# Hybrid decoder trunk on one core: the small transfers of gate offsets, router and gate columns held in program order

## The chip, the core and the metric

The kernel runs on one core of a Trainium2 chip. Its time is the device time of one execution in microseconds (us); lower is better. TensorE (PE) multiplies, VectorE (DVE) and ScalarE (ACT) do elementwise work, GpSimd (POOL) a few small things, and SyncE (SP) only issues transfers. ACT issues transfers too, between its other instructions. Transfers of SP run on the queue that the profile calls q1, those of ACT on q10.

## The reference, cut to what matters

Two layers on 256 tokens of width 1024. Each has a token mixer and a channel mixer (dense in layer 0, eight experts with a router in layer 1). The change touches the mixer's two small gate projections and constants beside them:

```python
p = h @ w_in
qk, v, o, ig, fg, cb, cc, cx, ga, gb = jnp.split(p, _split_points(), axis=-1)
qk = jax.nn.silu(causal_depthwise_conv(qk, conv_qk))
i_pre = (ig + b_gates[:H]).transpose(0, 2, 1)      # 4 heads: gate columns and gate offsets
f_pre = (fg + b_gates[H:]).transpose(0, 2, 1)
hm = mlstm_chunkwise(heads(q), heads(k) * (Dh ** -0.5), heads(v), i_pre, f_pre)
...
logits = (t @ w_router).astype(jnp.float32)        # layer 1 only
```

## The kernel before, in words

All products are made in three passes from a high and a low float32r part of each operand. Weights arrive as 1 MB units through SP into a ring of four buffers, `raw` (numbers 79 to 82 in the program's order). Each unit gives two halves. ACT casts a half to `hi` (line 121), DVE makes `lo` from the rest (line 123), both in rings of seven (hi_83 to hi_89, lo_90 to lo_96). PE then uses them.

The start, layer 0: the conditioning products (`ada_acc`, lines 275 and 277, sums on DVE in `accs`; `ada_col`, line 290 on PE and 292 on DVE, result `adac`) need four `w_ada` units and the table `badaT`, which PE turns (line 231) out of `prow`, a small transfer of ACT. `adac` scales the tokens: PE turns them (line 407), ACT and DVE apply the scale (399, 401), and the parts `h_hi`, `h_lo` (lines 80 and 81) go into the first large products (476 to 478, 464 to 466).

`mixer` then works through `w_in` in groups of 512 columns. After the first q/k group, `params()` has brought small tables: `prm` (convolution weights and norms, turned by PE at line 231 and copied at 232), the gate offsets `bg` (four transfers of 4 numbers each) and the router weights `wr` (128 partitions with eight runs of 8 numbers). `gates()` then borrows the next `hi` and `lo` tile (hi_89, lo_96) for the gate columns: a transfer brings `graw`, ACT casts it (502), DVE makes the low part (503), and PE makes 24 products (506 to 508). A chain of small steps on ACT and DVE follows, ending in `grow`, which PE turns at line 529 after the next group. In layer 1 the same `gates()` follows the last product for v.

A scheduler sets each engine's order from priorities and an estimate of readiness. It may move an instruction far ahead of where the code stands, unless it is wrapped in `tc.keep_in_program_order`, which keeps it behind the instructions of its engine that the code issued earlier. Completion of transfers is signalled on eight semaphores (DMAHW0 to DMAHW7 in the program's order), taken in turn by the transfers of both queues. A transfer waits until the earlier one on its semaphore has landed.

Of the kernel before, what the change touches and what calls it, by code (L numbers as in the profile page):

```python
# [46 lines left out]
def trunk(ctx: ExitStack, tc: tile.TileContext, x, c, w_ada, b_ada, w_in, w_gates, b_gates, conv_qk,  # L47
          hn_gain, conv_short, w_out, ln_g, ln_b, dense_w13, dense_w2, w_router, moe_w13,
          moe_w2, out):
    nc = tc.nc  # L50
# [12 lines left out]
    def bank(shape=(128, 512), name="bank"):  # L63
        return psum.tile(list(shape), F32, tag="bank", name=name)
# [21 lines left out]
    def turn(name):  # L86
        t = turns[name]
        t[0] += 1
        return t[1][t[0] % len(t[1])]
# [114 lines left out]
    def kview(w):  # L204
        return w.rearrange("(c p) n -> p c n", p=128)
# [20 lines left out]
    def rows_to_cols(t, n, srcs):  # L226
        r = small.tile([128, 512], F32, tag="hf", bufs=2, name="prow")[0:n, 0:128]
        for d, src in srcs:
            nc.scalar.dma_start(r[d], src)
        pt = bank()  # L230
        T.transpose(pt[:, 0:n], r, ident[0:n, 0:n])
        A.copy(t, pt[:, 0:n])
# [4 lines left out]
    bg = const.tile([64, 2], F32, name="bg")  # L237

    def params():
        V.memset(bg, 0.0)  # L240
        for l in range(2):
            rows_to_cols(prm[l], 128, [
                (slice(0, 64), conv_qk[l].rearrange("t (c p) -> (t c) p", p=128)),
                (slice(64, 88), conv_short[l].rearrange("t (c p) -> (t c) p", p=128)),
                (slice(88, 96), hn_gain[l].rearrange("(c p) -> c p", p=128)),
                (slice(96, 128), (ln_g, ln_b)[l].rearrange("l i (c p) -> (l i c) p", p=128))])
            if l == 1:
                nc.scalar.dma_start(wr, kview(w_router[0]))
            nc.scalar.dma_start(bg[0:4, l:l + 1], b_gates[l, 4:8].rearrange("(h o) -> h o", o=1))
            nc.scalar.dma_start(bg[32:36, l:l + 1], b_gates[l, 0:4].rearrange("(h o) -> h o", o=1))  # L250

    def lng_col(l, i):
        b = 96 + l * 16 + i * 8
# [3 lines left out]
    wr = const.tile([128, KC, NE], F32, name="wr")  # L257
# [233 lines left out]
    def gates(mix, l, hi, lo):  # L491

        gst_hi = turn("hi").rearrange("p (k m) -> p k m", m=128)
        gst_lo = turn("lo").rearrange("p (k m) -> p k m", m=128)
        G.memset(gst_hi.bitcast(F32), 0.0)
        G.memset(gst_lo.bitcast(F32), 0.0)
        grow = mix.tile([36, S], F32, name="grow")
        G.memset(grow, 0.0)
        gr = mix.tile([128, KC, 8], F32, name="graw")
        nc.scalar.dma_start(gr, w_gates[l])  # L500
        for src, dst in ((slice(4, 8), slice(0, 4)), (slice(0, 4), slice(32, 36))):
            A.copy(gst_hi[:, :, dst], gr[:, :, src])
            V.tensor_tensor(gst_lo[:, :, dst], gr[:, :, src], gst_hi[:, :, dst].bitcast(F32), op=OP.subtract)
        pg = bank()
        for k in range(KC):
            T.matmul(pg[:, 0:S], gst_hi[:, k], hi[:, k], start=k == 0, stop=False)
            T.matmul(pg[:, 0:S], gst_hi[:, k], lo[:, k], start=False, stop=False)
            T.matmul(pg[:, 0:S], gst_lo[:, k], hi[:, k], start=False, stop=k == KC - 1)

        f, e, bb, r = (mix.tile([4, S], F32, name=n) for n in ("gf", "ge", "gb", "gr"))  # L510
        M = f
        V.tensor_scalar(f, pg[0:4, 0:S], bg[0:4, l:l + 1], None, op0=OP.add)
        A.activation(r, pg[32:36, 0:S], AF.Identity, bias=bg[32:36, l:l + 1])
        V.scalar_tensor_tensor(e, f, -1.0, f, op0=OP.mult, op1=OP.min)
        A.activation(e, e, AF.Exp)
        A.activation(e, e, AF.Ln, bias=1.0)
        V.scalar_tensor_tensor(f, f, 0.0, e, op0=OP.min, op1=OP.subtract)
        V.tensor_tensor_scan(bb, ones[0:4, 0:1].to_broadcast([4, S]), f, 0.0, op0=OP.mult, op1=OP.add)
        V.tensor_tensor(r, r, bb, op=OP.subtract)
        V.tensor_tensor_scan(M, r, r, 0.0, op0=OP.max, op1=OP.max)  # L520
        V.tensor_tensor(e, bb, M, op=OP.add)
        V.tensor_copy(grow[0:4], r)
        A.activation(grow[32:36], e, AF.Exp, scale=-1.0)
        gcol = mix.tile([128, 2, 36], F32, name="gcol")

        def then():
            pc = bank((128, 2, 36))
            for tb in range(2):
                T.transpose(pc[:, tb], grow[:, tb * 128:tb * 128 + 128], ident[0:36, 0:36])
            V.tensor_copy(gcol, pc)  # L530
        return M, gcol, then
# [68 lines left out]
    def mixer(ctx, l, z, norms, Gc, Bc, xA, g1):  # L600
# [19 lines left out]
        if norms is None:  # L620
# [15 lines left out]
            for cg in range(2):  # L636
                for tb in range(2):
                    v_out(pvs[cg][tb], cg, tb)
            xA = xA(z)
            params()  # L640
        else:
            pvs = [[], []]
# [17 lines left out]
            background()  # L660
        lead[0] = AHEAD
        M, gcol, gates_then = gates(mix, l, hi, lo)
        q, k = t8("q"), t8("k")
        for gi in range(4):
# [917 lines left out]
```

## Time and profile before

| | |
|---|---|
| median of 3 runs | 1766.92 us (1766.28 to 1768.98) |
| the profiled execution, its own time | 1764.21 us |
| span in its trace | 1762.5 us |
| PE busy | 1669.0 us, 95% of the span |
| DVE, ACT, POOL busy | 1047.1, 719.6, 70.6 us |
| mean granted PE clock | 0.983 of full |

The span runs from the first to the last recorded instruction; the 1.7 us between it and the execution's own time lie around it. All rows below are of this one execution, in microseconds from the span's start.

### The profile page before, as it was taken

To read this page: it belongs to the slowest core of one execution; us is meant where nothing else is said; L and a number is where in the kernel's file an instruction comes from. 1 tells how busy PE (TensorE), PEld (TensorE's weight loads), DVE (VectorE), ACT (ScalarE), POOL (GpSimd) and SP (SyncE) were. 2 spreads that over 40 slices of the span, in tenths; PEclk is the share of its full clock that TensorE was granted. 3 is DMA by queue.
4 is the path that set the end of the run, shared out by engine and by line. 5 is a ranking of instruction groups with operands and counts; after the bars stand their busy time and mean duration, and the time that the engine had idled before them with its cause. 6 is when DMAs were issued, how large, how long until landed. Compare 5 with 4: busy or idle time off the path is not lost. (4 is left out here: it accounts for less than half of the span.)

```text
span 1762.5 us, 28144 instructions
## 1 busy us (share of the span) xinstructions
PE 1669.0 (95%) x11401; PEld 1282.6 (73%) x11401; DVE 1047.1 (59%) x1531; ACT 719.6 (41%) x975; POOL 70.6 (4%) x82
## 2 busy tenths in 40 slices
PE   5999998999998999997999999999999999999996
PEld 4899996999996999995776665555555555566662
DVE  7699858776567999758844644322323233555554
ACT  2774444544444764544633433222222222334440
POOL 0001002000003001003000000000000000000000
PEclk9999998999998999998999999999999999999998
DMA  8667753766663776662789999999899999999994
GB/s 342 222 250 267 263 181 123 283 249 253 229 236 123 286 268 256 242 229 107 263 330 416 411 397 376 373 403 380 352 419 364 393 393 411 392 366 421 421 420 175
DMA packets 78131, 541.16 MB, mean 307 GB/s; under 512 B 10057, under 2 KB 10409, under 8 KB 13225
## 3 DMA queue, kind: packets, MB, share of 16 engines
q1 hardware_dynamic: 74880, 534.81, 77.6%
q10 hardware_dynamic: 3112, 4.48, 0.7%
q8 instruction: 91, 1.49, 0.3%
q14 instruction: 48, 0.39, 0.1%
HBM read 538.20 MB, written 1.05 MB: 306 GB/s over the span
## 5 line engine op out<-in xcount | busy, mean ns | idle before, releaser
L123 DVE TENSOR_TENSOR lo<-raw,hi 128x1024 fp32r<-128x1024 f32 x376 | 449.7, 1220 | 162.7 <-ACT hi L121 162.2
L121 ACT CAST hi<-raw 128x1024 fp32r<-128x1024 f32 x382 | 389.8, 1048 | 273.3 <-PE grp L465 177.5
L464 PE MATMUL grp<-h_hi,hi 128*128 128x256 f32 x1408 | 401.8, 286 | 0.5 <-ACT hi L121 0.5
L466 PE MATMUL grp<-h_hi,lo 128*128 128x256 f32 x1408 | 397.7, 283 | 0.0
L465 PE MATMUL grp<-h_lo,hi 128*128 128x256 f32 x1408 | 397.5, 282 | 0.0
L464 PEld LDWEIGHTS grp<-h_hi,hi 128*128 128x128 f32 x1408 | 268.6, 191 | 2.9 <-issue 1.4
L465 PEld LDWEIGHTS grp<-h_lo,hi 128*128 128x128 f32 x1408 | 268.6, 191 | 2.0 <-issue 1.7
L466 PEld LDWEIGHTS grp<-h_hi,lo 128*128 128x128 f32 x1408 | 268.5, 191 | 0.0
L1132 DVE TENSOR_TENSOR ss<-bank,ss 128x256 f32<-128x256 f32 (+1 forms) x42 | 16.9, 402 | 236.7 <-PE bank L1085 236.7
L478 PE MATMUL bank<-lo,x_parts 128*128 128x512 f32 x336 | 137.2, 408 | 2.7 <-DVE lo L123 2.6
L476 PE MATMUL bank<-hi,x_parts 128*128 128x512 f32 x336 | 135.4, 403 | 2.8 <-ACT hi L121 2.8
L1130 ACT ACTIVATE ss<-bank 128x256 f32<-128x256 f32 (+1 forms) x42 | 15.4, 366 | 288.7 <-PE bank L1085 288.7
L477 PE MATMUL bank<-hi,x_parts 128*128 128x512 f32 x336 | 132.4, 394 | 0.0
L1085 PE MATMUL bank<-raw,x_pairs 128*64 128x256 f32 x1056 | 122.4, 385 | 0.0
L1085 PEld LDWEIGHTS bank<-raw,x_pairs 128*64 128x64 f32 x1056 | 74.3, 138 | 42.0 <-issue 3.4
L123 DVE TENSOR_TENSOR lo<-raw_moe,hi 128x1024 fp32r<-128x1024 f32 x76 | 89.5, 1220 | 25.0 <-ACT hi L121 24.9
L476 PEld LDWEIGHTS bank<-hi,x_parts 128*128 128x128 f32 x336 | 63.2, 188 | 31.7 <-ACT hi L121 19.5
L1085 PE MATMUL bank<-raw,mg 128*64 128x512 f32 (+1 forms) x432 | 85.6, 537 | 0.5 <-ACT mg L1145 0.5
L277 DVE SCALAR_TENSOR_TENSOR acc<-raw,cond,acc 128x512 f32<-128x512 f32 x120 | 83.7, 744 | 0.1
L121 ACT CAST hi<-raw_moe 128x1024 fp32r<-128x1024 f32 x76 | 76.3, 1050 | 14.7 <-PE bank L477 12.9
L478 PEld LDWEIGHTS bank<-lo,x_parts 128*128 128x128 f32 x336 | 63.0, 187 | 23.5 <-DVE lo L123 6.6
L1145 ACT COPY mg<-bank 128x256 f32<-128x256 f32 (+1 forms) x42 | 14.9, 355 | 158.3 <-PE bank L1142 158.3
(314 smaller groups left out, 2345.2 us busy)
## 6 DMA issues: line engine op xcount, KB each, us to landing
raw<-in_moe_w_dram SPq DMA_DIRECT2D x192, 1024.0 KB, 7.9
raw_moe<-in_moe_w_dram SPq DMA_DIRECT2D x96, 1024.0 KB, 7.2
raw<-in_w_in_dram SPq DMA_DIRECT2D x72, 1024.0 KB, 5.4
raw<-in_w_ada_dram SPq DMA_DIRECT2D x48, 1024.0 KB, 4.8
raw_big<-in_moe_w_dram SPq DMA_DIRECT2D x48, 1024.0 KB, 7.8
raw<-in_dense_w_dram SPq DMA_DIRECT2D x42, 1024.0 KB, 6.2
raw<-in_w_out_dram SPq DMA_DIRECT2D x8, 1024.0 KB, 5.8
g<-in_b_ada_dram SPq DMA_DIRECT2D x8, 256.0 KB
```

The source lines that it names most:

```text
L121: A.copy(hi, raw)
L123: V.tensor_tensor(lo, raw, hi.bitcast(F32), op=OP.subtract)
L277: V.scalar_tensor_tensor(a, raw[:, jj], cond[:, j:j + 1], a, op0=OP.mult, op1=OP.add)
L464: T.matmul(o, whi[:, kk, fs], hi[:, k], start=first, stop=False, skip_group_check=True)
L465: T.matmul(o, whi[:, kk, fs], lo[:, k], start=False, stop=False, skip_group_check=True)
L466: T.matmul(o, wlo[:, kk, fs], hi[:, k], start=False, stop=k == KC - 1, skip_group_check=True)
L476: T.matmul(o, ahi, whi, start=start, stop=False)
L477: T.matmul(o, alo, whi, start=False, stop=False)
L478: T.matmul(o, ahi, wlo, start=False, stop=stop)
L1085: T.matmul(o[c * p:c * p + p, 0:n], act, w[:, c * n:c * n + n], start=start, stop=stop)
L1130: A.activation(dst, src, AF.Silu)
L1132: V.tensor_tensor(dst, src, dst, op=OP.mult)
```

## The change

Six transfers are wrapped: the router weights, the four gate offsets (the two lines become a loop over the same two slices) and, in each layer, the gate columns. What is moved, and how many bytes, stays the same.

```diff
             if l == 1:
-                nc.scalar.dma_start(wr, kview(w_router[0]))
-            nc.scalar.dma_start(bg[0:4, l:l + 1], b_gates[l, 4:8].rearrange("(h o) -> h o", o=1))
-            nc.scalar.dma_start(bg[32:36, l:l + 1], b_gates[l, 0:4].rearrange("(h o) -> h o", o=1))
+                tc.keep_in_program_order(nc.scalar.dma_start(wr, kview(w_router[0])))
+            for ps, hs in ((slice(0, 4), slice(4, 8)), (slice(32, 36), slice(0, 4))):
+                tc.keep_in_program_order(
+                    nc.scalar.dma_start(bg[ps, l:l + 1], b_gates[l, hs].rearrange("(h o) -> h o", o=1)))
...
         gr = mix.tile([128, KC, 8], F32, name="graw")
-        nc.scalar.dma_start(gr, w_gates[l])
+        tc.keep_in_program_order(nc.scalar.dma_start(gr, w_gates[l]))
```

Lines below 249 have numbers one higher in the changed kernel. Three places of the order show what moves.

On SP at the start, with the semaphores that each transfer waits for, before:

```order
L114 DMA raw_80<-in_w_ada_dram 128x2048
L114 DMA raw_81<-in_w_ada_dram 128x2048
L114 DMA raw_82<-in_w_ada_dram 128x2048
L114 DMA raw_79<-in_w_ada_dram 128x2048 [waits DMAHW4_49]
L114 DMA raw_80<-in_w_in_dram 128x2048 [waits DMAHW5_49,DMAHW1_49,DVE_49]
```

and in the changed kernel:

```order
L114 DMA raw_80<-in_w_ada_dram 128x2048
L114 DMA raw_81<-in_w_ada_dram 128x2048
L114 DMA raw_82<-in_w_ada_dram 128x2048
L114 DMA raw_79<-in_w_ada_dram 128x2048
L114 DMA raw_80<-in_w_in_dram 128x2048 [waits DMAHW1_49,DVE_49]
```

The order is the same; the fourth load no longer waits for a semaphore that a transfer of ACT's held.

On ACT in layer 0, from the copies of the two `prm` tables on. Before, where the six transfers stand far ahead, five of them at the start of the program and the sixth behind `badaT`:

```order
L232 COPY prm_120<-bank 128x128
L232 COPY prm_121<-bank 128x128
L541 ACTIVATE q<-cpad_132,prm_120 128x256 x2
L536 COPY cpad_133<-grp 128x2x256
L541 ACTIVATE q<-cpad_133,prm_120 128x256 x2
L121 CAST hi_89<-raw_81 128x1024
L513 ACTIVATE gr<-bank,bg 4x256
```

and in the changed kernel:

```order
L232 COPY prm_120<-bank 128x128
L251 DMA bg<-in_b_gates_dram 4x1 x2
L232 COPY prm_121<-bank 128x128
L248 DMA wr<-in_w_router_dram 128x8x8
L251 DMA bg<-in_b_gates_dram 4x1 x2
L501 DMA graw<-in_w_gates_dram 128x64
L542 ACTIVATE q<-cpad_132,prm_120 128x256 x2
L537 COPY cpad_133<-grp 128x2x256
L542 ACTIVATE q<-cpad_133,prm_120 128x256
L503 CAST hi_89<-graw 128x8x4 x2
```

All six transfers and the cast of the gate columns now stand behind the copy of `prm_120`. PE's order here is unchanged: the two turns of `prm` (line 231), then the 24 gate products that read hi_89, then the next group.

On ACT in layer 1, around the copies of v. Before, where `graw` was asked for some 340 us earlier:

```order
L617 COPY v_ext<-bank 128x2x256
L502 CAST hi_89<-graw 128x8x4 x2
L617 COPY v_ext<-bank 128x2x256 x2
L121 CAST hi_83<-raw_82 128x1024
L121 CAST hi_84<-raw_82 128x1024
```

and in the changed kernel:

```order
L618 COPY v_ext<-bank 128x2x256 x3
L501 DMA graw<-in_w_gates_dram 128x64
L121 CAST hi_83<-raw_82 128x1024
L121 CAST hi_84<-raw_82 128x1024
L503 CAST hi_89<-graw 128x8x4 x2
```

The transfer is now issued behind the last copy of v, and its cast stands two casts later. On PE the first two gate products still come directly behind the last product for v; seven instead of four products of the next group now stand between them and the other 22.

## Rows read from the trace of the kernel before

**Rows 1.** From the page: span, and busy time of each engine.

```profile
span 1762.5 us, 28144 instructions
PE 1669.0 (95%) x11401; PEld 1282.6 (73%) x11401; DVE 1047.1 (59%) x1531; ACT 719.6 (41%) x975; POOL 70.6 (4%) x82
```

**Rows 2.** Two waits of PE from 60 to 800 us, that is from the first q/k group to the experts; columns are engine, line, what it waited for, then us in total, times, longest.

```profile
PE bank L477 <- DVE h_lo L81: 9.3, 4, 3.9
PE bank L529 <- ACT grow L523: 0.6, 1, 0.6
```

**Rows 3.** SP's queue in the first 14.3 us in order of time (start, length of the row, count), and SP's longest wait in that time from the view of waits.

```profile
0.82 1.34 SPq L114 DMA_DIRECT2D raw<-in_w_ada_dram  x3
13.93 0.33 SPq L114 DMA_DIRECT2D raw<-in_w_ada_dram  x1
SPq L114 <- DMA prow<-in_b_ada_dram: 11.8, 1, 11.8
```

**Rows 4.** ACT in order of time in the same stretch; ACTq rows are transfers that it issues.

```profile
5.95 0.34 ACTq L229 DMA_DIRECT2D prow<-in_b_ada_dram  x1
6.33 0.57 ACTq L249 DMA_DIRECT2D bg<-in_b_gates_dram  x1
6.93 0.26 ACTq L250 DMA_DIRECT2D bg<-in_b_gates_dram  x1
7.22 0.40 ACTq L248 DMA_DIRECT2D wr<-in_w_router_dram  x1
...
14.49 0.36 ACTq L500 DMA_DIRECT2D graw<-in_w_gates_dram  x1
```

**Rows 5.** PE (first four) and DVE (last two) in order of time, 14 to 29 us; in brackets the idle time before the row and what ended it.

```profile
14.05 0.39 PE L231 MATMUL bank<-ident,prow 96*128 96x96 f32 x1 [14.05 <-DMA prow<-in_b_ada_dram]
14.24 3.67 PE L290 MATMUL bank<-ones,accs 128*128 128x128 f32 x16
20.88 0.49 PE L290 MATMUL bank<-ones,accs 128*128 128x128 f32 x2 [2.96 <-DVE accs L277]
...
28.34 1.31 PE L476 MATMUL bank<-hi,h_hi 128*128 128x512 f32 x2 [2.61 <-ACT h_hi L80]
18.03 0.16 DVE L292 SCALAR_TENSOR_TENSOR adac<-bank,badaT 128x4 f32<-128x4 f32 x1 [2.07 <-PE bank L290]
18.75 0.75 DVE L277 SCALAR_TENSOR_TENSOR accs<-raw,cond,accs 128x512 f32<-128x512 f32 x1 [0.56 <-DMA raw<-in_w_ada_dram]
```

**Rows 6.** PE, then ACT, around the gate products of layer 0, in order of time; the last PE row is the first product of the next group.

```profile
70.67 0.38 PE L231 MATMUL bank<-ident,prow 128*128 128x128 f32 x2
70.81 0.36 PE L506 MATMUL bank<-h_hi,hi 128*128 128x256 f32 x1
...
73.74 0.28 PE L464 MATMUL grp<-h_hi,hi 128*128 128x256 f32 x1
71.71 0.43 ACT L232 COPY prm<-bank 128x128 f32<-128x128 f32 x2
```

**Rows 7.** The load that SP issues in that stretch, and the transfer engines there: slices of 1 us with busy time (and instruction count) of PE, PEld, DVE, ACT and POOL, then granted PE clock, share of the 16 transfer engines, GB/s.

```profile
73.09 0.33 SPq L114 DMA_DIRECT2D raw<-in_w_in_dram  x1
73.00:74.00 1.00, 1.00 (x11) 1.00 (x10) 1.00 (x4) 0.97 (x3) 0.00 (x0) 1.00 0.00 0
74.00:75.00 1.00, 1.00 (x11) 1.00 (x10) 1.00 (x4) 1.00 (x2) 0.00 (x0) 1.00 0.80 156
...
77.00:78.00 1.00, 1.00 (x11) 1.00 (x10) 1.00 (x3) 0.97 (x3) 0.00 (x0) 1.00 0.13 41
```

**Rows 8.** Small transfers that shared the engines with a load: ACT's first and last of the eight that bring `prow` (the last one waits for the first one's semaphore); then packets, MB and share of 16 engines of SP's queue q1 from 54.5 to 58.5 us, where q10 has no row, and of q10 from 58.5 to 60 us.

```profile
55.06 0.53 ACTq L229 DMA_DIRECT2D prow<-in_conv_qk_dram  x1
...
59.73 0.32 ACTq L229 DMA_DIRECT2D prow<-in_ln_b_dram  x1
q1 hardware_dynamic: 146, 1.13, 77.4%
q10 hardware_dynamic: 312, 0.12, 28.4%
```

**Rows 9.** The cast of the gate columns (both halves) in layer 1, from ACT in order of time.

```profile
570.49 0.34 ACT L502 CAST hi<-graw 128x32 fp32r<-128x32 f32 x2
```

**Rows 10.** Two stretches without PE work, each followed by the products behind it: length, PE busy (count), granted PE clock, transfer share, GB/s.

```profile
25.80:28.30 2.50, 0.00 (x0) 1.00 1.03 416
28.30:31.60 3.30, 3.26 (x7) 0.50 0.87 345
555.40:559.60 4.20, 0.46 (x1) 0.74 0.00 0
559.60:564.20 4.60, 4.60 (x11) 0.50 0.21 34
```

**Rows 11.** Layer 1 around its gate products: PE, ACT's last copy of v, SP's load in flight, and one slice of 1 us with columns as in rows 7.

```profile
581.22 0.68 PE L506 MATMUL bank<-h_hi,hi 128*128 128x256 f32 x1
582.55 0.39 PE L464 MATMUL grp<-h_hi,hi 128*128 128x256 f32 x1 [0.53 <-ACT hi L121]
580.97 0.59 ACT L617 COPY v_ext<-bank 128x512 f32<-128x512 f32 x1 [4.90 <-PE bank L478]
579.20 0.33 SPq L114 DMA_DIRECT2D raw<-in_w_in_dram  x1
583.00:584.00 1.00, 0.86 (x8) 0.69 (x7) 1.00 (x3) 1.00 (x2) 0.00 (x0) 1.00 0.18 74
```

## The prediction

> **What bounds the kernel now.** I read the shares first: PE is busy for 1669.0 of 1762.5 us [rows 1], so a stretch counts only by what it does to PE. The waits of PE over both mixers come next [rows 2]. There the reader sees almost nothing: 9.3 us behind the normalizations, where PE waits for steps that follow its own results, and 0.6 us for `grow`. PE runs layer 0's mixer without a break, so a stall put there is not made good by slack that it has today, and a start that comes earlier is kept too. Then three places, in order of time: the start, the gate products of layer 0, and those of layer 1.
>
> At the start SP issues three `w_ada` loads by 2.2 us and the fourth at 13.93; the wait is 11.8 us, for `prow` to land [rows 3]. The order shows why: that load shares a completion semaphore with this transfer of ACT's. In layer 0, PE turns `prm` at 70.67 and goes straight on to the gate products at 70.81 [rows 6], since `graw` has long been there: it was issued at 14.49 [rows 4].
>
> **The change, part by part.** *Start.* Without the five transfers ahead, the semaphores fall otherwise and the fourth `w_ada` load can be issued near 2.2 us. It now lands at about 18.75, when DVE's wait of 0.56 us ends [rows 5]. But DVE has the first `adac` at 18.03 ahead of it, which waits for 16 products of PE; those started at 14.24, behind the turn of `prow` at 14.05, and took 3.67 us [rows 5]. `prow` is not moved, nor is the 1 MB of tokens that stands ahead of it on ACT's queue. So the sums start at 18.19 instead of 18.75, and the large products at 28.34 [rows 5] come 0.56 us earlier: **-0.6 us**. Of the 11.8 us this is all that reaches PE. It could be more if `prow` also lands earlier, because the router's small runs no longer follow it: up to another 1.0 us, the lower bound being -1.6. The upper bound is 0.
>
> *Layer 0.* ACT's copy of `prm` starts at 71.71 and the pair takes 0.43 us [rows 6]. Behind the first copy ACT now issues two `bg`, behind the second `wr`, two `bg` and `graw`. The prices of an issue are 0.57 and 0.26 for `bg`, 0.40 for `wr`, 0.36 for `graw`, with 0.03 between two [rows 4]. Copies until about 72.1; four `bg` at the mean of 0.42 are 1.7, `wr` 0.4, with the gaps: `graw` is issued at 74.0 to 74.4 (from 73.6 if each `bg` takes 0.26, to 75.0 if each takes 0.57). I take 74.1.
>
> When it lands is the main unknown. SP issues a 1 MB load at 73.09; the slice up to 74 has no traffic, the next three are full, and it is done at 77.1 [rows 7], so about 1 us passes from issue to the first bytes. `wr` and this load come up together, with `graw` behind both. The nearest row is `prow` of the tables: issued at 55.06, and ACT's last transfer of the eight, which waits for its semaphore, could go at 59.73, so it took 4.6 us. Until 58.5 only SP's queue moved data, 1.13 MB; the 312 small packets of ACT's came after it [rows 8]. By that row `graw` moves after 77.1 and has landed at about 77.8. Two casts of together 0.34 us follow [rows 9], so the gate products start at 78.2 instead of 70.81 [rows 6]: **+7.4 us**, in which PE stands. Lower bound: with nothing ahead, issue at 73.6, 1 us to the first bytes, 1 us to move and signal, 0.4 for the casts: 76.0, that is 5.2 us. Upper bound: issue at 75.0, 4.6 us as in rows 8, another 0.9 for the small runs of `wr`, the casts: 80.9, that is 10.1 us. The casts stand behind `graw` on ACT with the silu steps and the cast of hi_89 queued behind; they are needed later than the gate products, and hi_89 can't be overwritten before these anyway.
>
> The granted clock is added to that. After 2.5 us without work the next 3.3 us were granted 0.50, after 4.2 us nearly without work the next 4.6 us [rows 10]: 1.2 instead of 2.4 GHz, so half of 3.3 to 4.6 us is lost. After 7 us of standing I take **+1.9 us** (0 to 2.3). Against it stands the wait for `grow`, 0.6 us [rows 2]: the chain still starts behind the gate products, but its order on ACT now has fewer silu steps between its parts, so I let it end in time: **-0.6 us** (0 at worst).
>
> *Layer 1.* The last copy of v starts at 580.97 [rows 11], so `graw` is issued near 581.5 instead of long before. The load in flight was issued at 579.20; its traffic ends in the slice 583 to 584, which is 0.18 full [rows 11]. `graw` can move in that gap and land at about 584.0. The two casts of weights ahead of its own end by then, and with 0.4 us for its casts PE goes on at 584.4 to 584.5 instead of at 581.22: 3.3 us. PE loses some of that here already: between 581.74 and the first low-part product it does four products of 0.12 us and stands 0.53 us for a cast [rows 11], in all 0.9 us that the longer wait swallows. Left are 2.4 us, and the clock on top: the stand of 2.6 us is as long as that of 2.5 us which cost 1.65 [rows 10]; I take half, 0.8. **+3.2 us**, from 1.5 (landed at 583.2, clock kept) to 6.7 (4.6 us to land as in rows 8, and 2.3 for the clock).
>
> *Hidden.* The transfer taken away at 229 us saves ACT 0.36 us on an engine that is 41% busy, so nothing. SP's loads between 75 and 130 us change semaphores and places, and some now wait for the small transfers to land; these are in by 80 us, and the ring still holds the next group's weights, four halves of `hi`. I price it at 0; if that cover failed, PE would wait for a 1 MB load, some 3 to 4 us by rows 7.
>
> **Sum.** -0.6 + 7.4 + 1.9 - 0.6 + 3.2 = **+11.3 us**. The profiled execution took 1764.2 us (span 1762.5), so it would take 1775.5; it lies 2.7 us below the median of the runs shown, and on the median the sum gives **1778 us**. All terms at their low ends give +4.5 (-1.6 + 5.2 + 0 - 0.6 + 1.5), all at their high ends +19.1 (0 + 10.1 + 2.3 + 0 + 6.7).
>
> **A rule that would change the stall.** In layer 0 the forecast lets `graw` wait for SP's whole load, as the small packets of rows 8 did. The Trainium skill ("DMA: Bandwidth & Descriptors", section on queues, rings and completion order) says that each transfer engine takes turns between the queues that have work, packet by packet, so a small transfer would not stand behind another queue's load. The row speaks against it: for 3 us none of ACT's packets moved.
>
> **Rivals.** *Turns are taken.* If ACT's queue gets its turn in the middle of the load, `graw` moves at about 75.4 behind `wr` and lands at 76.2; PE goes on at 76.6, 5.8 us late instead of 7.4: +9.7, 1776.6 us. For it: q10 and q1 shared the engines at the start. Against it: rows 8. Chance 0.25; the forecast as summed has 0.45.
>
> *The new semaphore order hurts as well.* Loads that now wait on `bg`, `wr` or `graw` come late for the second or third group, and PE waits once or twice more for 3 to 4 us: 1782 to 1785 us. Against it: the ring's cover. Chance 0.18.
>
> *Hidden after all.* PE's added waits come back from the waits behind the normalizations. Those follow PE's own last products, so I see no way for it except small stalls all around: `graw` near its low bound in both layers and the clock kept, 1768 to 1770 us. Chance 0.07.
>
> *Faster.* The early load was the true bound: if the whole start hung on SP's wait, the large products would come up to 11.8 us earlier [rows 3], and the sum would be 11.9 without the start's term, less 11.8: 1767.0 us. It ends faster from the point where the start gains more than the 11.9 us that the two gate products cost, by 3.5 us more to be told from no change, as with these at the lower prices above. The idle rows speak against it: at 14.05 PE waited for `prow`, and `adac` waited for PE. Chance 0.05.
>
> **Range and chances.** The measurement tells about 0.2%, 3.5 us, from no change. The first three cases (0.88) all lie beyond 1770.5, so slower 0.88, within 0.2% 0.07, faster 0.05. The range that leaves out no more than 2 in 10 runs from 1769.5, near the low ends, to 1786, the high ends: it takes in the price of each unknown landing.
>
> **What would show it.** Right: SP's fourth `w_ada` load issued before 3 us and the large products only about half a us earlier; in layer 0 a row at the first gate product with some 7 us idle, released by ACT's cast of `graw`, and half the clock behind it; no wait for `grow`; in layer 1 some 3 us idle at the same line. Wrong, if `graw` lands within 2 us of its issue in both layers, if the large products start several us earlier than 27.8, or if PE shows new waits for casts of weights between 85 and 130 us.

## The result: slower by 13 us

| | before | after |
|---|---|---|
| median, runs beside each other | 1766.01 us (1763.46 to 1768.98, 6 runs) | 1779.08 us (1776.06 to 1782.9, 6 runs) |
| ratio, with its 95% interval | | 1.0075 [1.0062, 1.0088] |
| profiled execution: own time, span | 1764.21, 1762.5 us | 1778.52, 1776.7 us |

A second set of runs of the changed kernel (the last of the experiments' repeats below) gave 1.0088 [1.0073, 1.0103]. The profiled execution is 14.3 us longer than that of before. The prediction's sum was +11.3, and its time 1778.0.

Where the 14.3 us arise is read from when PE comes to the same product in both traces. The third column of times is a second profile of the same changed kernel, which tells how much of a shift belongs to the kernel and how much to one execution.

| PE comes to | before | after (shift) | after, second profile (shift) |
|---|---|---|---|
| turn of `prow` for `badaT` | 14.05 | 16.03 (+2.0) | 15.6 (+1.6) |
| first large product | 28.34 | 29.96 (+1.6) | 28.84 (+0.5) |
| turn of `prm`, ahead of layer 0's gates | 70.67 | 73.43 (+2.8) | 72.53 (+1.9) |
| first gate product, layer 0 | 70.81 | 82.25 (+11.4) | 80.9 (+10.1) |
| turn of `grow` | 86.0 | 98.7 (+12.7) | 97.8 (+11.8) |
| first gate product, layer 1 | 581.22 | 597.05 (+15.8) | 596.42 (+15.2) |
| last gate product of high parts, layer 1 | 585.8 | 602.6 (+16.8) | 599.9 (+14.1) |
| router | 814.4 | 830.9 (+16.5) | 828.2 (+13.8) |
| last expert's second product | 1747.3 | 1761.4 (+14.1) | 1761.4 (+14.1) |

### The profile after

The page's span and busy time: PE works no longer than in [rows 1], 1669.5 against 1669.0 us. Of the 14.2 us that the span grew, 13.7 are time in which PE stands. What it loses by half the clock behind the gates is made up elsewhere: the mean granted clock is 0.984, and was 0.983.

```profile
span 1776.7 us, 28160 instructions
PE 1669.5 (94%) x11401; PEld 1284.8 (72%) x11401; DVE 1048.5 (59%) x1531; ACT 719.8 (41%) x973; POOL 69.5 (4%) x82
```

PE's waits from 60 to 800 us, as [rows 2]: a new first line, the casts of the gate columns. The wait for `grow` is gone.

```profile
PE bank L507 <- ACT hi L503: 12.6, 2, 8.4
...
```

The start in order of time: SP's queue, PE, then DVE, as [rows 3, 5].

```profile
0.82 2.17 SPq L114 DMA_DIRECT2D raw<-in_w_ada_dram  x4
8.99 7.68 SPq L114 DMA_DIRECT2D raw<-in_w_in_dram  x3
...
16.03 0.40 PE L231 MATMUL bank<-ident,prow 96*128 96x96 f32 x1 [16.03 <-DMA prow<-in_b_ada_dram]
...
29.96 1.25 PE L477 MATMUL bank<-hi,h_hi 128*128 128x512 f32 x3 [2.19 <-ACT h_hi L80]
20.01 0.16 DVE L293 SCALAR_TENSOR_TENSOR adac<-bank,badaT 128x4 f32<-128x4 f32 x1 [3.69 <-PE bank L291]
```

SP's wait of 11.8 us is gone: all four `w_ada` loads are out by 3 us. But `prow` lands 2 us later, and PE's 16 products behind it and DVE's first `adac` (18.03 before, 20.01 now) move with it. The queues show why. Packets, MB and share of the transfer engines of both queues in the slices 12 to 13 and 13 to 14 us:

```profile
q1 hardware_dynamic: 57, 0.35, 84.8%
q10 hardware_dynamic: 48, 0.07, 20.0%
...
q1 hardware_dynamic: 49, 0.39, 93.4%
q10 hardware_dynamic: 49, 0.02, 8.6%
```

Before, the same two slices were:

```profile
q10 hardware_dynamic: 575, 0.13, 59.7%
q1 hardware_dynamic: 34, 0.15, 36.2%
...
q10 hardware_dynamic: 634, 0.02, 35.7%
```

While SP waited, ACT's queue had the engines nearly for itself, and `prow` and the router's runs passed within the two slices. Now SP's loads go on. In the second slice one packet of q1 passes for each of q10, 49 and 49, and those of q1 are of 8 KB (0.39 MB in 49). At 49 small packets per us the 96 rows of `prow` (128 numbers, 512 bytes each) take 2 us, and that is the delay.

The gates of layer 0, from ACT and then PE in order of time, as [rows 4, 6]:

```profile
73.75 0.85 ACTq L251 DMA_DIRECT2D bg<-in_b_gates_dram  x2
...
74.66 0.40 ACTq L248 DMA_DIRECT2D wr<-in_w_router_dram  x1
...
75.43 0.60 ACTq L251 DMA_DIRECT2D bg<-in_b_gates_dram  x2
76.07 0.36 ACTq L501 DMA_DIRECT2D graw<-in_w_gates_dram  x1
...
81.76 0.34 ACT L503 CAST hi<-graw 128x32 fp32r<-128x32 f32 x2 [3.25 <-DMA graw<-in_w_gates_dram]
82.25 0.55 PE L507 MATMUL bank<-h_hi,hi 128*128 128x256 f32 x1 [8.43 <-ACT hi L503]
```

`graw` is issued 2.6 us behind PE's turn of `prm`, and 5.7 us pass until its cast can start. Three slices of the queues, 75 to 77, 77 to 80 and 80 to 82 us, tell where those went:

```profile
q1 hardware_dynamic: 11, 0.09, 36.7%
q10 hardware_dynamic: 1064, 0.03, 27.8%
...
q1 hardware_dynamic: 114, 0.92, 82.3%
q10 hardware_dynamic: 23, 0.01, 0.9%
...
q10 hardware_dynamic: 121, 0.03, 6.3%
q1 hardware_dynamic: 19, 0.04, 5.2%
```

First the 1064 packets of which `wr` makes up 1024, then SP's 1 MB load, and only behind it the bulk of `graw`. PE stands 8.4 us, and its clock drops on top. Length, PE busy (count), granted clock, transfer share and GB/s of the stand and of the products behind it:

```profile
73.40:82.20 8.80, 0.41 (x4) 0.66 0.56 171
82.20:86.60 4.40, 4.36 (x21) 0.51 0.00 0
```

Layer 1, ACT and PE in order of time, as [rows 11]; the last row is the slice of 5 us behind the stand, with its granted clock:

```profile
592.11 0.59 ACT L618 COPY v_ext<-bank 128x512 f32<-128x512 f32 x1 [4.90 <-PE bank L479]
592.12 0.33 ACTq L501 DMA_DIRECT2D graw<-in_w_gates_dram  x1
...
596.57 0.34 ACT L503 CAST hi<-graw 128x32 fp32r<-128x32 f32 x2 [1.99 <-DMA graw<-in_w_gates_dram]
597.05 0.55 PE L507 MATMUL bank<-h_hi,hi 128*128 128x256 f32 x1 [4.12 <-ACT hi L503]
...
597.00:602.00 5.00, 4.95 (x23) 0.51 0.81 292
```

### The profile page after: what moved, and what is told of

Its sections match the earlier page's. It is cut to its first block, busy times and chain, and to the rows that moved or that the text cites. A ratio compares the mean times of both kernels' runs of the same rounds, so it can differ in the third digit from the quotient of the medians.

```text
span 1776.7 us, 28160 instructions
## 1 busy us (share of the span) xinstructions
PE 1669.5 (94%) x11401; PEld 1284.8 (72%) x11401; DVE 1048.5 (59%) x1531; ACT 719.8 (41%) x973; POOL 69.5 (4%) x82
```

## The experiments

Each run is compared with runs of the kernel before on the same chip. Their median was 1764.62 us (19 runs) for the first four experiments below. It was 1764.59 (29 runs) for the gate columns at the mixer's start, the swap on top of that (first set), the swap in the kernel before, and the changed kernel again. It was 1766.19 (23 runs) for the second set of that swap and the swap with the tables held. Theory: the two stands at the gates, caused by asking for `graw` late and behind other packets, are nearly the whole cost, and the start costs a little because `prow` lands late. Rivals: the order of the semaphores or the held tables cost something of their own; the start's loss is carried to the end in full.

### Tables held, gate columns free

```diff
-        tc.keep_in_program_order(nc.scalar.dma_start(gr, w_gates[l]))
+        nc.scalar.dma_start(gr, w_gates[l])
```

> Only the gate offsets and the router weights are held; the gate columns stay early in both layers. If the later turn of prow (16.03 instead of 14.05 us) comes from the fourth w_ada load, which is now issued near 2 us and shares the transfer engines with prow, the large products of layer 0 start 1.5 to 3 us later than before and nothing stands at the gate products: 1768 to 1769 us, +2 to +3 on before. If that late start was chance in one profile, or is made good before the gate products, the time is that of before, 1766 us.

Measured: 1765.21 us (11 runs), ratio 1.0007 [0.9996, 1.0017]. `prow` lands late here too, and there is no wait for gate columns; PE's waits from 60 to 800 us keep `grow` (1.0 us). PE's turn of `prow`:

```profile
15.66 0.39 PE L231 MATMUL bank<-ident,prow 96*128 96x96 f32 x1 [15.66 <-DMA prow<-in_b_ada_dram]
```

The five small tables held in order can't be told from no change (at most 3 us by the interval), so the order of semaphores that comes with them costs nothing that shows. All but at most 3 of the 13 us belong to the gate columns. Of the start, 0.7 us arrive at the first large product and 2.1 at the first product of the next group, yet only 0.5 at the last expert's second product.

### Gate columns held in layer 1 alone

```diff
+        d = nc.scalar.dma_start(gr, w_gates[l])
+        if l == 1:
+            tc.keep_in_program_order(d)
```

(the other five as before)

> Only layer 1's gate columns are held. PE should stand about 4 us at the first gate product of layer 1 and run 4 to 5 us at half clock behind it, which the changed kernel's trace puts at +5.4 us in all at that place. If all of it reaches the end: 1771.5 us. If the experts' loads, which have run ahead meanwhile, give part of it back, as the distance between the two traces suggests (16.5 us at the router, 14.2 at the end): 1769 us, +3.

Measured: 1769.53 us (8 runs), 1.0027 [1.0015, 1.0039]: +4.7 us by the ratio. PE at layer 1's first gate product, and the 5 us behind it with their granted clock:

```profile
588.26 0.55 PE L508 MATMUL bank<-h_hi,hi 128*128 128x256 f32 x1 [4.51 <-ACT hi L504]
...
588.00:593.00 5.00, 4.74 (x22) 0.50 0.70 254
```

ACT issues `graw` at 582.93 and it lands 4.85 us later, while SP's loads go on. Layer 1 alone costs 4 to 5 us in the runs. The profile's own +5.3 holds +1.9 that was there ahead of the gates. From the last copy of v to the router its shift grows from +1.9 to +8.0, so the gates cost 6.1 us in this trace, and 2.7 come back in the experts.

### Gate columns asked for ahead of the router weights

In layer 0 `params` asks for `graw` between the first two `bg` and `wr`; all is still held.

```diff
...
-            params()
+            gr = params(lambda: gate_columns(mix, l))
...
```

> All is held as in the changed kernel, but in layer 0 the gate columns are asked for ahead of the router weights and of the last two gate offsets. If in the changed kernel their packets waited behind the router's small runs and SP's 1 MB load, they now land within about 2.5 us of the issue, near 77 us, and PE stands 3.5 to 4 us there instead of 8.4: 1774 us. If a small transfer on ACT's queue takes some 5.6 us to land whatever stands ahead, only the earlier issue counts, 1.4 us: 1777.7 us.

Measured: 1776.11 us (5 runs), 1.0062 [1.0049, 1.0076]. ACT's issue and cast, and PE's first gate product:

```profile
74.19 0.36 ACTq L496 DMA_DIRECT2D graw<-in_w_gates_dram  x1
...
76.82 0.32 ACT L508 CAST hi<-graw 128x32 fp32r<-128x32 f32 x2
77.28 0.55 PE L512 MATMUL bank<-h_hi,hi 128*128 128x256 f32 x1 [3.88 <-ACT hi L508]
```

Ahead of `wr` and of SP's load the same transfer is there within 2.6 us instead of 5.7, and the stand is 3.9 instead of 8.4 us. Of the 4.5 us that the stand is shorter, 3.1 are the quicker landing and about 1.5 the earlier issue (1.2 us behind the turn of `prm` instead of 2.6). So the place in the queue is over a third of layer 0's stand, as the theory had it. The time falls by less, to between the two times expected. The intervals of this kernel and of the changed one overlap, so the runs alone don't tell them apart, and its profile (1774.36) is the shortest of its five runs.

### The changed kernel with the start's table ahead of the tokens

```diff
-    nc.scalar.dma_start(z, x[0].rearrange("(t p) d -> p t d", p=128))
     ... (table badaT)
+    nc.scalar.dma_start(z, x[0].rearrange("(t p) d -> p t d", p=128))
```

> The changed kernel with the 48 KB transfer for badaT issued ahead of the 1 MB of tokens on ACT's queue. If the start hangs on prow, its turn moves from 16 to about 8 us, the first conditioning products start when their sums are done (12.5), the fourth w_ada load (landed near 16) is used at once, and the large products start near 26 to 27 us instead of 29.96: 1775 to 1776 us. If the start hangs on the weight loads alone: 1779 us, as the changed kernel.

Measured: 1774.81 us (6 runs), 1.0065 [1.0049, 1.0081]. PE at the start (the tokens `z` are `z_in` in the profile):

```profile
8.25 0.39 PE L230 MATMUL bank<-ident,prow 96*128 96x96 f32 x1 [8.25 <-DMA prow<-in_b_ada_dram]
...
25.80 1.74 PE L477 MATMUL bank<-hi,h_hi 128*128 128x512 f32 x3 [2.61 <-ACT h_hi L80]
```

With `prow` early the large products come 4.2 us earlier than in the first profile of the changed kernel (3.0 than in the second), so its start does hang on `prow`. The span is 6.2 us shorter, and the medians, from separate sets of runs, differ by 4.3. But measured against before the ratios are 1.0065 and 1.0075, with intervals that overlap, and two of the six runs lie at 1780. How much of the start reaches the end in this pair isn't shown.

### Gate columns at the mixer's start, all held

```diff
+            gr = gate_columns(mix, l)
...
-        M, gcol, gates_then = gates(mix, l, hi, lo)
+        M, gcol, gates_then = gates(mix, l, hi, lo, gr)
```

> The gate columns (graw) are asked for at the start of each mixer instead of where the gates begin; all small transfers are still held in the order of the code on ACT's queue. If the stands before the gate products are the cost of the change, both are gone (no stand over 1 us on hi there), the start's delay of 1 to 2 us is mostly made good as in the run with the parameters alone, and the time is 1764.5 to 1766.5 us beside 1764.6 before. If the late offsets bg and router weights wr, or the new order as such, cost something of their own, it stays above 1768.

Measured: 1767.2 us (12 runs, 1764.22 to 1770.18), 1.0010 [1.0000, 1.0019]: between the two expectations, but next to the first. Both stands are gone. The profiled execution (1769.48, near the top of its runs) is at +4.2 us at the first gate product already, though its first large product comes only 0.5 us late. Between the two lie a long start below the full clock and a second such stretch at 56 us:

```profile
28.80:36.80 8.00, 7.04 (x17) 0.58 0.62 216
56.20:61.00 4.80, 4.70 (x13) 0.64 0.72 270
```

Five of its runs lie at 1764.2 to 1765.7 and seven at 1767.1 to 1770.2. That fits stretches that come in some executions and not in others, but only one of the twelve was profiled. Whether the late tables cost a us of their own isn't settled by this run; the last two runs bear on it.

### The start's table first, in three kernels

The same swap as above: in the kernel before; on top of the gate columns at the mixer's start (run twice); on top of the tables held and gate columns free.

> The kernel before with the swap alone: prow is issued ahead of z, nothing is held. SP's fourth load of in_w then still waits for a small transfer on the shared semaphore, but for another one, so the start depends on which: if the first large product hangs on prow and on the bank of the parameters' transpose, it starts at about 26 us and the time is that of the run with swap and early gate columns (1761 to 1762). If it hangs on SP's fourth load, which waits for the tokens, it starts at about 28 and the time stays at 1764 to 1765.

> As the run with the gate columns asked for early, and the first parameter transfer (prow) is issued ahead of the 1 MB of tokens (z). From the swap alone in the changed kernel: prow's transpose at about 8.3 us, the first large product at about 25.8 instead of 28.3. If a gain at the start is carried to the end it is 2.5 to 4 us faster than before, 1761 to 1762. If early gains are made good later like early losses (of 1.6 us 0.5 was left), it is about 1764, no difference.

> The run with the parameters alone held (graw free, so asked for right behind prow), with prow issued ahead of z. As with swap and early gate columns the fourth load doesn't wait and prow lands early: prow's transpose at 8.3 us, first large product at 25.9, no stands at the gates. If those alone set the time it is the same as with the gate columns held at the mixer's start: 1762 to 1763. If the 2 us between the run with early gate columns (1767.2) and that with the parameters alone (1765.2) come from the later offsets and the held graw, it is 2 us less than that: 1760 to 1761.

> The kernel with the gate columns at the mixer's start and prow ahead of z once more, beside the one above and new runs of before: 1761.5 to 1763.5, faster than before by 1 to 3 us. If the gain was chance, no difference.

| swap in | time | ratio to before |
|---|---|---|
| kernel before | 1764.93 us (11 runs) | 0.9995 [0.9986, 1.0004] |
| gate columns at the mixer's start | 1762.53 us (12 runs) | 0.9987 [0.9979, 0.9996] |
| the same, second set | 1763.3 us (12 runs) | 0.9990 [0.9981, 1.0000] |
| tables held, gate columns free | 1761.96 us (12 runs) | 0.9980 [0.9971, 0.9990] |

In the kernel before, `prow` is there at 8.3 us too, and nothing comes of it. SP's longest waits and PE at the first large product, from that kernel:

```profile
SPq L114 <- DMA bg<-in_b_gates_dram: 7.0, 2, 6.6
...
28.20 1.74 PE L476 MATMUL bank<-hi,h_hi 128*128 128x512 f32 x3 [4.90 <-ACT h_hi L80]
```

SP waits for another small transfer instead, and the large products stay at 28.2. With the tables held and the gate columns free, SP's queue and PE's turn of `prow`:

```profile
0.82 2.06 SPq L114 DMA_DIRECT2D raw<-in_w_ada_dram  x4
...
8.41 0.39 PE L230 MATMUL bank<-ident,prow 96*128 96x96 f32 x1 [8.41 <-DMA prow<-in_b_ada_dram]
```

Both limits had to go together: SP's early load is worth nothing while `prow` is late, an early `prow` nothing while SP waits. With both, the large products start at 26.0 instead of 28.34, and by the three ratios 2 to 4 us are kept to the end (the second set's interval reaches to no change). The last kernel is the fastest here: 0.2% below the kernel before, with an interval that leaves out no change. The two variants differ from each other by less than their intervals, so the place of the gate columns, once they are early, isn't told apart here.

### The changed kernel again

> The changed kernel once more, beside the others of this call: 1776 to 1779 us, stands of about 8.4 us at the first layer's gates and 4 us at the second's. Its spread tells how far a few us between the experiments can be read.

Measured: 1780.32 us (4 runs), 1.0088 [1.0073, 1.0103], above the time expected. PE's waits from 60 to 800 us have the same first line:

```profile
PE bank L507 <- ACT hi L503: 10.3, 2, 8.0
```

The total, 14.1 us at the last product, is the same as in the first profile, though the parts differ: layer 1's stand was 2.3 us instead of 4.1, shorter than expected (here `graw` landed within 2.7 us), and the experts gave nothing back.

## Why the prediction was right, and where its steps failed

The forecast held: +13.1 us between the medians against +11.3, by the cause it named, and the time lies 1.1 us from 1778. That it came so close is in part luck. In the first profile the terms missed by +3.4 (start), +1.3 (layer 0's stand), -1.6 (layer 0's rest), +2.2 (layer 1's gates) and -2.4 us (experts), which leaves +2.9. The terms, one by one (first profile, with the second's in brackets):

| term | forecast | measured |
|---|---|---|
| start | -0.6 | +2.8 (+1.9) |
| stand at layer 0's gates | +7.4 | +8.7 (+8.2) |
| clock behind it, less `grow`'s wait | +1.9 - 0.6 | +1.3 (+1.7) |
| layer 0's rest and normalizations, to the end of v | 0 | -1.6 (+0.5) |
| layer 1's gates | +3.2 | +5.4 (+1.5) |
| channel mixer's router to the end | 0 | -2.4 (+0.3) |

**Start: wrong sign.** The step that failed is "`prow` is not moved, nor is the 1 MB of tokens that stands ahead of it", and with it the bound that only a gain was possible. `prow` was not moved in its queue, but SP's loads, which the old wait had held back, now moved beside it. The forecast asked what the freed load would wait for, and not what it would collide with. Then the slow products grew, from seven in 3.3 us before [rows 10]. In the first profile of the changed kernel PE made three products, stood 0.89 us for `h_lo` and made the next eight at half the clock; in the second profile 14 were slow (the rows stand in the last section). That is why +1.6 at the first product became +2.8 by 73 us. The prediction also had it that PE keeps what the start gains or loses. In the trace of the run with the tables alone 2.1 us at the next group are 0.5 at the last expert's second product, and its time can't be told from no change: at most 3 us by its interval.

**Layer 0: right, a little small.** Issue, queue and casts went as worked out. `graw` was issued at 76.07; less the start's shift that is 73.3, ahead of the 74.1 taken. The landing was mis-sized: 5.7 us instead of 3.7. `wr` took 75 to 77 us with its 1024 packets, the load followed until about 80 us, and the bulk of `graw` came last. The forecast had the small runs of `wr` (0.9 us) in the upper bound alone. The run that asks for `graw` ahead of `wr` and load takes away 4.5 us of the stand, 3.1 of them by the quicker landing.

**The rival "turns are taken" fell in layer 0, and held at the start.** From 77 to 80 us 23 packets of q10 passed beside 114 of q1 in the first profile: no turns one by one. The Trainium skill ("DMA: Bandwidth & Descriptors", section on queues, rings and completion order) says that the engines take turns packet by packet between queues. The trace agrees at the start, where q10 and q1 moved 49 packets each in 1 us, and there it costs the small transfer 2 us. In layer 0 the first profile doesn't show it. The second shows it for one us, 78 to 79, late in the load; `graw` still took 5.3 us from issue to cast there:

```profile
q1 hardware_dynamic: 48, 0.39, 93.3%
q10 hardware_dynamic: 46, 0.01, 5.1%
```

In layer 1 of the first profile, q10 has no packet at all from 593 to 595 us, 1 to 3 us behind the issue of `graw`:

```profile
q1 hardware_dynamic: 102, 0.84, 100.2%
```

What sets these places apart was not tried and stays open. One difference in the rows: at the start ACT's queue was busy without a break when SP's load came, and in layer 0 `graw` was issued (76.07) within 0.3 us of SP's load (its issue ends at 76.18, and one takes 0.33 us as in [rows 7]). In layer 1 it was issued into a stream of SP's loads.

**Clock and `grow`: right.** The stretch behind the stand had 0.51 of the clock for 4.4 us [rows 10 had 3.3 and 4.6], so 2.2 us, and the wait of 0.6 us went away.

**Layer 0's rest: not foreseen.** From the turn of `grow` to the end of v the shift fell by 1.6 us in the first profile and rose by 0.5 in the second. In that stretch PE's longest wait for `h_lo` ahead of layer 1's products was 2.6 us in the first profile, and 3.9 in the second and before. Why it differs between executions stays open.

**Layer 1: mis-sized.** The forecast let `graw` move in a gap and land 2.5 us after its issue. It took 4.5 us in the first profile and 4.85 in the run with layer 1 alone, behind SP's loads, and 5 us at half the clock followed. The second profile has the shorter landing that was forecast, so both happen: 2.3 and 4.1 us of standing for one kernel. By the runs with layer 1 alone it is +4.7 us, within the bounds given (1.5 to 6.7). The 0.9 us that the forecast let the wait swallow counts four products, which are work in either kernel; only PE's standing among them could be swallowed.

**The experts: not foreseen, and not a reserve.** In the first profile 2.4 us came back behind the router. That looks like slack; the granted clock says otherwise. Length, PE busy (count), clock, share, GB/s in the same two stretches, before and then after:

```profile
860.00:866.00 6.00, 5.88 (x26) 0.72 0.64 266
1340.00:1360.00 20.00, 18.36 (x122) 0.91 0.84 317
```

```profile
860.00:866.00 6.00, 6.00 (x27) 1.00 0.47 176
1340.00:1360.00 20.00, 17.74 (x145) 1.00 0.96 386
```

Before lost 0.28 of 6 us and 0.09 of 20 us there, 3.5 us in all, and after none. The second profile of the changed kernel has 0.97 in 860 to 920 us and 0.98 in 1300 to 1400, the same as before has there, and gives nothing back. Layer 1 alone has 1.00 in both and gives 2.7 back. So it goes with the clock in four profiles. It was not forced by an experiment.

**Chances.** "Semaphore order hurts" fell: no wait for casts of weights appears between 85 and 130 us, and the tables alone cost nothing. "Hidden" fell. "Faster" named a true thing, in part: the start could come earlier once SP doesn't wait, but by 2.3 us, not 11.8, and only with `prow` moved as well.

## What to carry to other kernels

A transfer that has landed early for free should stay early: held in program order it is asked for where it is needed, and pays its issue, the small packets ahead of it and another queue's megabyte in a row (5.7 us here, 2.6 without the last two), and then half a clock. When a wait is taken from one queue, look at what its transfers will move beside: the freed 1 MB load cost the small table 2 us. Where two things limit a start, take away both before judging either; here each alone showed nothing, and together they gave 2 to 4 us.

## What the runs showed of the hardware that was not expected

- Two queues at once, packet by packet: 49 small packets and 49 of 8 KB in the same us, so that a transfer of 96 rows takes 2 us beside a stream of loads. At two other places a small transfer that was issued beside a load or into a stream of loads moved little or nothing for 2 to 3 us.
- The same kernel starts with a different number of slow products. The stretch at 0.50 of the clock (1.2 GHz) at the start was 3.3 us before [rows 10], and in the second profile of the changed kernel:

```profile
28.80:35.00 6.20, 6.16 (x14) 0.50 0.60 197
```

  In the first profile PE made three products at full clock, stood 0.89 us and made eight at 0.50:

```profile
29.90:31.60 1.70, 1.23 (x3) 1.00 0.00 0
32.10:35.30 3.20, 3.20 (x8) 0.50 0.90 307
```

  The Trainium skill ("TensorE: Matmul & The Clock Gate", Part 1) says that the number of slow products at a start varies from run to run of one kernel; the two profiles of the changed kernel agree (8 and 14 slow products).
- Half-clock stretches inside the experts come in some executions and not in others, at a cost of 1.7 and 1.8 us in the profile of before. With them and the slow products at the start, a difference of 2 to 4 us between two single profiles is no evidence; here only medians of many runs, or a row that names the wait, decided.
